# A Winograd-style 3x3 convolution: whole-image stores, whole-pair loads and one shared pool of 16 KB slots

## The chip, the cores and the metric

The kernel runs on one core of a Trainium2 chip. The metric is the device time of one execution in microseconds (us); lower is better. The kernel before takes 131.04 us, the median of 10 runs (130.84 to 131.21).

A core has five engines with a queue of instructions each: TensorE (PE in the profile, with its weight loads as PEld) multiplies matrices into eight PSUM banks; VectorE (DVE), ScalarE (ACT) and GpSimd (POOL) work element by element; SyncE (SP) issues transfers. Sixteen transfer engines move data between the chip's main memory (DRAM in the names) and SBUF, the memory on the core with 128 partitions. Transfers are issued here from SP, from ACT and from POOL; each of these has a queue of its own.

## The reference

The reference is a 3x3 convolution with zero padding, in fp32, on 16 images of 64 channels and 64 x 64 pixels, with 128 output channels:

```python
x_pad = np.pad(x, ((0, 0), (0, 0), (1, 1), (1, 1)), mode='constant')
for b in range(batch):
    for co in range(c_out):
        for ci in range(c_in):
            for kh in range(3):
                for kw in range(3):
                    output[b, co] += weight[co, ci, kh, kw] * x_pad[b, ci, kh:kh+h, kw:kw+w]
```

The input is 16.8 MB, the output 33.6 MB.

## The kernel before

**Tiling.** Two images make a pair: 2 x 64 input channels fill the 128 partitions. There are eight pairs (`NP`). A pair is computed in four blocks of eight double rows (16 output rows). Each image of the pair uses its own half of the partitions as contraction, so products for the two images alternate on PE.

**The arithmetic of a block.** Even and odd output rows share a part. With G0, G1 and G2 the weights of the three kernel rows, the kernel makes `U`, the product of G1 with the sum of the two rows of a double row (`ss`); `A`, the products of G2 - G1 (`G21`) and G0; and `Bt`, those of G0 - G1 (`G01`) and G2. The even output row is U + A and the odd one U + Bt. `group` issues the products: 6 for `U`, 12 for each of the other two, 30 a block. ACT copies `U` to SBUF as `ut` (L158), four buffers; DVE adds `A` and `ut` for both images (L163), then `Bt` and `ut` (L166), into the output tile `ot`. Then SP stores each image's 16 rows, 512 KB (L167), 4 KB in one piece per partition. `opool` has 16 such `ot` tiles of 8 KB per partition, which is four images' worth.

**Inputs.** All products use fp16. Pair 0 is loaded as fp32 (`x0`) in four cuts of rows, the first on ACT's queue and the rest on SP's, and ACT casts it to `xs[0]`. Pairs 1 to 7 are loaded by GpSimd's queue in halves (L56), with the cast done in the transfer. All eight fp16 pairs have a buffer of their own, so that no load waits for one. `load(p + 4)` is issued from GpSimd's program at the top of pair p.

**Row sums.** `ss` is made by DVE for pair 0 from `x0` and by GpSimd for the others from `xs` (L74), one pair ahead, in three buffers.

**Start.** The weights are loaded (SP), cast (L87), transposed by PE (L94) and combined into `Wt` by ACT and DVE (L96 to L104).

**Order.** A tile scheduler orders the program by engine and gives out the slots of the pools; `keep_in_program_order` (here `keep`) fixes the order of the calls it wraps. Every engine takes its instructions in order, and SP issues its transfers in order too. Each transfer on SP or ACT also uses one of eight completion semaphores in turn, and is issued when the earlier transfer on the same one has landed.

Of the kernel before, what the change touches and what calls it, by code (L numbers as in the profile page):

```python
# [8 lines left out]
F32 = mybir.dt.float32  # L9
F16 = mybir.dt.float16  # L10


@with_exitstack
def kernel(
    ctx: ExitStack,
    tc: tile.TileContext,
    x: bass.AP,
    weight: bass.AP,
    out: bass.AP,
):  # L20
    nc = tc.nc
    B, CI, H, W = x.shape
    CO = weight.shape[0]
    assert H == 64 and W == 64 and CI == 64 and CO == 128 and B % 2 == 0
    NP = B // 2
    RB = 8

    keep = tc.keep_in_program_order
    x_rows = x.rearrange("b c h w -> (b c) h w")
    out_rows = out.rearrange("b co h w -> b co h w")  # L30
    w_flat = weight.rearrange("co ci kh kw -> co (ci kh kw)")

    const = ctx.enter_context(tc.tile_pool(name="const", bufs=1))
    psum = ctx.enter_context(tc.tile_pool(name="psum", bufs=8, space=bass.MemoryType.PSUM))
    xpool = ctx.enter_context(tc.tile_pool(name="xpool", bufs=1))
    opool = ctx.enter_context(tc.tile_pool(name="opool", bufs=16))
    spool = ctx.enter_context(tc.tile_pool(name="spool", bufs=3))
    upool = ctx.enter_context(tc.tile_pool(name="upool", bufs=4))


    w_raw = const.tile([CO, CI * 9], F32)
    nc.sync.dma_start(w_raw, w_flat)  # L42
    x0 = const.tile([128, H, W], F32)
    xs = [
        xpool.tile([128, H, W], F16, tag=f"xs{p}", name="xs") for p in range(NP)
    ]
    cuts = [(0, 18), (18, 34), (34, 50), (50, 64)]
    for n, (lo, hi) in enumerate(cuts):
        eng = nc.scalar if n == 0 else nc.sync
        eng.dma_start(x0[:, lo:hi, :], x_rows[0:128, lo:hi, :])  # L50
    ident = const.tile([128, 128], F16)

    def load(p):
        for lo in (0, 32):
            keep(
                nc.gpsimd.dma_start(  # L56
                    xs[p][:, lo : lo + 32, :],
                    x_rows[128 * p : 128 * p + 128, lo : lo + 32, :],
                )
            )  # L60

    make_identity(nc, ident)
    for p in range(1, 4):
        load(p)


    ss = {}

    def sums(eng, p, src, lo, n):
        if p not in ss:  # L70
            ss[p] = spool.tile([128, H // 2, W], F16, tag="ss", name="ss")
        v = src.rearrange("p (j i) c -> p j i c", i=2)
        keep(
            eng.tensor_add(  # L74
                ss[p][:, lo : lo + n, :], v[:, lo : lo + n, 0, :], v[:, lo : lo + n, 1, :]
            )
        )


    Wt = const.tile([128, 5, 3, CO], F16)  # L80
    G0, G21, G1, G01, G2 = range(5)

    def wrow(i):
        return Wt[:, i, :, :].rearrange("p t c -> p (t c)")

    w16 = const.tile([CO, CI * 9], F16)
    nc.vector.tensor_copy(w16, w_raw)  # L87
    wps = {}
    for kh in (1, 2, 0):
        wp = psum.tile([128, 512], F32, tag="acc", name="wp")  # L90
        for k in range(3):
            t = 3 * kh + k
            for q in (0, 64):
                nc.tensor.matmul(wp[q : q + 64, k * CO : k * CO + CO], w16[:, t::9], ident)  # L94
        wps[kh] = wp[:, 0 : 3 * CO]
    keep(nc.scalar.copy(wrow(G1), wps[1]))  # L96
    sums(nc.vector, 0, x0, 0, RB)
    keep(nc.vector.tensor_sub(wrow(G21), wps[2], wrow(G1)))  # L98
    keep(nc.vector.tensor_sub(wrow(G01), wps[0], wrow(G1)))  # L99
    for n, (lo, hi) in enumerate(cuts):  # L100
        keep(nc.scalar.copy(xs[0][:, lo:hi, :], x0[:, lo:hi, :]))  # L101
        if n == 0:
            keep(nc.scalar.copy(wrow(G0), wps[0]))  # L103
            keep(nc.scalar.copy(wrow(G2), wps[2]))  # L104
        if n < 3:
            sums(nc.vector, 0, x0, RB * (n + 1), RB)

    for p in range(NP):
        if p + 1 < NP:
            for lo in (0, 16):  # L110
                sums(nc.gpsimd, p + 1, xs[p + 1], lo, 16)
        if p + 4 < NP:
            load(p + 4)
        for blk in range(4):
            j0 = blk * RB

            def group(wi_rows):

                tiles = [
                    psum.tile([128, RB, W], F32, tag="acc", name="acc") for _ in range(2)  # L120
                ]
                n = 3 * len(wi_rows)
                i = 0
                for wi, off in wi_rows:
                    for kw in (1, 0, 2):
                        c_lo, c_hi = max(0, 1 - kw), min(W, W + 1 - kw)
                        for b2 in range(2):
                            p0 = 64 * b2
                            lo, hi = j0, j0 + RB
                            if off is None:  # L130
                                rhs = ss[p][p0 : p0 + 64, lo:hi, c_lo + kw - 1 : c_hi + kw - 1]
                            else:
                                while 2 * lo + off < 0:
                                    lo += 1
                                while 2 * (hi - 1) + off > H - 1:
                                    hi -= 1
                                first = 2 * lo + off
                                last = 2 * (hi - 1) + off
                                rhs = xs[p][
                                    p0 : p0 + 64,  # L140
                                    first : last + 1 : 2,
                                    c_lo + kw - 1 : c_hi + kw - 1,
                                ]
                            nc.tensor.matmul(  # L144
                                tiles[b2][:, lo - j0 : hi - j0, c_lo:c_hi],
                                Wt[p0 : p0 + 64, wi, kw, :],
                                rhs,
                                start=i == 0,
                                stop=i == n - 1,
                            )  # L150
                        i += 1
                return tiles

            U = group([(G1, None)])
            us = []
            for b2 in range(2):
                ut = upool.tile([128, RB, W], F32, tag="ut", name="ut")
                nc.scalar.copy(ut, U[b2])  # L158
                us.append(ut)
            ots = [opool.tile([128, RB, 2, W], F32, tag="ot", name="ot") for _ in range(2)]  # L160
            A = group([(G21, 1), (G0, -1)])
            for b2 in range(2):
                nc.vector.tensor_add(ots[b2][:, :, 0, :], A[b2], us[b2])  # L163
            Bt = group([(G01, 0), (G2, 2)])
            for b2 in range(2):
                nc.vector.tensor_add(ots[b2][:, :, 1, :], Bt[b2], us[b2])  # L166
                nc.sync.dma_start(  # L167
                    out_rows[2 * p + b2, :, blk * 16 : blk * 16 + 16, :],
                    ots[b2].rearrange("p j i c -> p (j i) c"),
                )  # L170


# [28 lines left out]
```

## Time and profile before

| what | before |
|---|---|
| median of 10 runs | 131.04 us (130.84 to 131.21) |
| the profiled execution's own time | 130.91 us |
| its span | 129.1 us |
| PE busy (products) | 107.0 us, 83% |
| DVE busy | 86.8 us, 67% |
| ACT busy | 40.8 us, 32% |
| POOL busy | 37.7 us, 29% |
| moved by the transfer engines | 43.44 MB, mean 336 GB/s |
| read from and written to main memory | 17.07 and 33.55 MB, 392 GB/s over the span |
| stores, 64 of 512 KB, median from issue to landing | 10.5 us |
| loads with cast, 14 of 512 KB (as written), median to landing | 15.2 us |

The span is the time from the first to the last record of the profiled execution on the core; 1.8 us of the execution lie outside of it. The profile divides the span into 40 slices of 3.2 us and shows the busy share of each engine per slice in tenths, then the granted clock of PE, the share of the transfer engines, and the GB/s moved. For a load with cast the GB/s count the bytes written, half of those read. The chain of work that ended last is followed back from the last instruction; by line, half of the span on it is PE's products (L144) and 20% a store of `ot`.

### The profile page before, as it was taken

To read this page: it belongs to the slowest core of one execution; us is meant where nothing else is said; L and a number is where in the kernel's file an instruction comes from. 1 tells how busy PE (TensorE), PEld (TensorE's weight loads), DVE (VectorE), ACT (ScalarE), POOL (GpSimd) and SP (SyncE) were. 2 spreads that over 40 slices of the span, in tenths; PEclk is the share of its full clock that TensorE was granted. 3 is DMA by queue.
4 is the path that set the end of the run, shared out by engine and by line. 5 is a ranking of instruction groups with operands and counts; after the bars stand their busy time and mean duration, and the time that the engine had idled before them with its cause. 6 is when DMAs were issued, how large, how long until landed. Compare 5 with 4: busy or idle time off the path is not lost.

```text
span 129.1 us, 2506 instructions
## 1 busy us (share of the span) xinstructions
PE 107.0 (83%) x978; PEld 55.8 (43%) x978; DVE 86.8 (67%) x135; ACT 40.8 (32%) x72; POOL 37.7 (29%) x34
## 2 busy tenths in 40 slices
PE   0099269999999999898999999999999999995000
PEld 0053035555555555354555555555555555552000
DVE  0262599787778777169988777877777777778000
ACT  3084273333333333331333333333333333330000
POOL 7404699691049105700092009200000000000000
PEclk9999999999999999999999999999999999999755
DMA  3999999999999999999999999999999999999950
GB/s 73 361 287 269 242 204 222 274 277 279 277 273 279 286 273 278 287 414 420 415 414 424 412 420 416 412 420 420 414 415 420 418 419 412 419 418 418 420 245 14
DMA packets 11963, 43.44 MB, mean 336 GB/s; under 512 B 1328, under 2 KB 1328, under 8 KB 11952
## 3 DMA queue, kind: packets, MB, share of 16 engines
q1 hardware_dynamic: 9792, 35.36, 68.7%
q0 software_dynamic: 2016, 7.34, 28.1%
q10 hardware_dynamic: 144, 0.59, 1.4%
q8 instruction: 7, 0.11, 0.3%
q14 instruction: 4, 0.03, 0.1%
HBM read 17.07 MB, written 33.55 MB: 392 GB/s over the span
## 4 chain that ended last, share of the span: by engine, by line
PE 50%; DMA 31%; DVE 4%; issue 3%; ACT 2%; SPq 1%; ACTq 1%; DVEq 1%
PE acc L144 50%; DMA out_dram<-ot 20%; DMA x<-in_x_dram 10%; DVE ot L163 2%; ACT ut L158 1%; DVE ot L166 1%; ACT xs L101 1%; ACTq L196 1%; SPq L50 1%; DVEq L196 0%; SPq L42 0%; DVEq L163 0%; ACTq L158 0%
## 5 line engine op out<-in xcount | busy, mean ns | idle before, releaser
L144 PE MATMUL acc<-xs,Wt 64*128 64x504 f16 (+3 forms) x768 | 95.1, 378 | 4.8 <-ACT ut L158 3.4
L144 PEld LDWEIGHTS <-Wt 64*128 64x128 f16 x960 | 54.7, 95 | 55.5 <-issue 8.4
L163 DVE TENSOR_TENSOR ot<-acc,ut 128x512 f32<-128x512 f32 x64 | 41.5, 685 | 21.6 <-ACT ut L158 14.0
L158 ACT COPY ut<-acc 128x512 f32<-128x512 f32 x64 | 34.3, 589 | 65.7 <-issue 53.2
L74 POOL TENSOR_TENSOR ss<-xs 128x1024 f16<-128x1024 f16 x14 | 29.5, 2124 | 43.1 <-issue 26.4
L166 DVE TENSOR_TENSOR ot<-acc,ut 128x512 f32<-128x512 f32 x64 | 41.0, 683 | 0.0
L144 PE MATMUL acc<-ss,Wt 64*128 64x504 f16 (+1 forms) x192 | 32.4, 384 | 0.0
L74 DVE TENSOR_TENSOR ss<-x 128x512 f16<-128x512 f32 x4 | 5.4, 1350 | 4.5 <-DMA x<-in_x_dram 4.4
L56 POOL DMA_DIRECT2D xs<-in_x_dram x14 | 7.7, 561 | 0.1
L94 PE MATMUL wp<-ident,w 128*64 128x128 f16 x18 | 1.3, 328 | 6.3 <-DVE w L87 6.3
L101 ACT CAST xs<-x 128x1024 f16<-128x1024 f32 (+2 forms) x4 | 4.2, 1049 | 4.3 <-DMA x<-in_x_dram 4.3
L87 DVE CAST w<-w_raw 128x576 f16<-128x576 f32 x1 | 0.5, 460 | 5.8 <-DMA w_raw<-in_weight_dram 5.8
L94 PEld LDWEIGHTS <-w 128*64 128x64 f16 x18 | 1.1, 210 | 6.3 <-DVE w L87 6.3
L96 ACT CAST Wt<-wp 128x384 f16<-128x384 f32 x1 | 0.5, 479 | 4.5 <-PE wp L94 4.5
L96 ACT ACT_TABLE_LOAD x1 | 1.3, 1283 | 1.2 <-PEq L185 1.2
L98 DVE TENSOR_TENSOR Wt<-wp,Wt 128x384 f16<-128x384 f32 x1 | 0.6, 558 | 0.5 <-ACT Wt L96 0.5
L99 DVE TENSOR_TENSOR Wt<-wp,Wt 128x384 f16<-128x384 f32 x1 | 0.5, 547 | 0.0
L103 ACT CAST Wt<-wp 128x384 f16<-128x384 f32 x1 | 0.5, 479 | 0.0
L104 ACT CAST Wt<-wp 128x384 f16<-128x384 f32 x1 | 0.5, 484 | 0.0
masks.py:199 POOL TENSOR_SCALAR_AFFINE_SELECT ident<-ident 128x128 f16<-128x128 f16 x1 | 0.3, 294 | 0.1
masks.py:197 POOL MEMSET ident<- 128x128 f16 x1 | 0.2, 206 | 0.3 <-POOLq L185 0.3
L185 POOL MEMSET const-float32-0.0<- 128x1 f32 x1 | 0.1, 99 | 0.2 <-issue 0.2
(3 smaller groups left out, 0.3 us busy)
## 6 DMA issues: line engine op xcount, KB each, us to landing
out_dram<-ot SPq DMA_DIRECT2D x64, 512.0 KB, 10.5
xs<-in_x_dram POOLq DMA_DIRECT2D x14, 512.0 KB, 15.2
x<-in_x_dram SPq DMA_DIRECT2D x2, 512.0 KB, 8.7
x<-in_x_dram ACTq DMA_DIRECT2D x1, 576.0 KB, 5.5
x<-in_x_dram SPq DMA_DIRECT2D x1, 448.0 KB, 13.5
w_raw<-in_weight_dram SPq DMA_DIRECT2D x1, 288.0 KB, 5.0
```

The source lines that it names most:

```text
L50: eng.dma_start(x0[:, lo:hi, :], x_rows[0:128, lo:hi, :])
L56: nc.gpsimd.dma_start(xs[p][:, lo : lo + 32, :], x_rows[128 * p : 128 * p + 128, lo : lo + 32, :],)
L74: eng.tensor_add(ss[p][:, lo : lo + n, :], v[:, lo : lo + n, 0, :], v[:, lo : lo + n, 1, :])
L94: nc.tensor.matmul(wp[q : q + 64, k * CO : k * CO + CO], w16[:, t::9], ident)
L96: keep(nc.scalar.copy(wrow(G1), wps[1]))
L98: keep(nc.vector.tensor_sub(wrow(G21), wps[2], wrow(G1)))
L101: keep(nc.scalar.copy(xs[0][:, lo:hi, :], x0[:, lo:hi, :]))
L144: nc.tensor.matmul(tiles[b2][:, lo - j0 : hi - j0, c_lo:c_hi], Wt[p0 : p0 + 64, wi, kw, :], rhs, start=i == 0, stop=i == n - 1,)
L158: nc.scalar.copy(ut, U[b2])
L163: nc.vector.tensor_add(ots[b2][:, :, 0, :], A[b2], us[b2])
L166: nc.vector.tensor_add(ots[b2][:, :, 1, :], Bt[b2], us[b2])
L196: with _tile.TileContext(nc) as tc:
```

## The change

- **Loads.** All pairs are loaded as fp32 on SP's queue. Pair 0 comes in its four cuts, the others in one transfer each, 2 MB with 16 KB per partition. No load casts any more; `cast` does it on ACT in four pieces per pair, spread over the blocks of one to three pairs ahead of use (the lists `casts`). The weights' load goes to ACT's queue.
- **Row sums** on GpSimd are made from the fp32 pair.
- **Buffers.** A pool `big` has nine slots of 16 KB per partition. Incoming fp32 pairs (`xf`) and whole output images (`ot`) take them in turn. The fp16 pairs `xs` have three slots instead of eight.
- **Stores.** Both images of a pair are stored after its last block, each in one transfer of 2 MB with 16 KB per partition; the last pair in two halves per image.
- **Order on SP.** The source issues loads 0 to 5 at the start, load 6 at the end of pair 0 and load 7 at the end of pair 2, each ahead of the pair's stores. The scheduler takes the slots from those that are free.

The core of the diff, with the line numbers left out:

```diff
-    xpool = ctx.enter_context(tc.tile_pool(name="xpool", bufs=1))
-    opool = ctx.enter_context(tc.tile_pool(name="opool", bufs=16))
+    xpool = ctx.enter_context(tc.tile_pool(name="xpool", bufs=3))
+    big = ctx.enter_context(tc.tile_pool(name="big", bufs=9))
...
-    nc.sync.dma_start(w_raw, w_flat)
+    nc.scalar.dma_start(w_raw, w_flat)
...
     def load(p):
-        for lo in (0, 32):
+        xf[p] = big.tile([128, H, W], F32, tag="big", name="xf")
+        for lo, hi in cuts if p == 0 else [(0, H)]:
             keep(
-                nc.gpsimd.dma_start(
-                    xs[p][:, lo : lo + 32, :],
-                    x_rows[128 * p : 128 * p + 128, lo : lo + 32, :],
+                nc.sync.dma_start(
+                    xf[p][:, lo:hi, :], x_rows[128 * p : 128 * p + 128, lo:hi, :]
                 )
             )
+    def cast(p, n):
+        if p not in xs:
+            xs[p] = xpool.tile([128, H, W], F16, tag="xs", name="xs")
+        lo, hi = cuts[n]
+        keep(nc.scalar.copy(xs[p][:, lo:hi, :], xf[p][:, lo:hi, :]))
+    def outs(p):
+        ots[p] = [big.tile([128, H // 2, 2, W], F32, tag="big", name="ot") for _ in range(2)]
+    for p in range(5):
+        load(p)
+    outs(0)
+    load(5)
...
+    pieces = lambda q: [(q, n) for n in range(4)]
+    casts = {p: [] for p in range(NP)}
+    casts[0] = pieces(1)
+    casts[1] = pieces(2) + pieces(3)[:2]
+    casts[2] = pieces(3)[2:] + pieces(4)
+    casts[3], casts[4], casts[5] = pieces(5), pieces(6), pieces(7)
...
-            for lo in (0, 16):
-                sums(nc.gpsimd, p + 1, xs[p + 1], lo, 16)
-        if p + 4 < NP:
-            load(p + 4)
+        if p not in ots:
+            outs(p)
+        for q, _ in dict.fromkeys((q, 0) for q, _ in casts[p]):
+            if q not in ss:
+                for lo in (0, 16):
+                    sums(nc.gpsimd, q, xf[q], lo, 16)
...
-                nc.scalar.copy(ut, U[b2])
+                keep(nc.scalar.copy(ut, U[b2]))
...
+            if p == 0 and blk < 3:
+                cast(0, blk + 1)
+            c = casts[p]
+            for q, n in c[len(c) * blk // 4 : len(c) * (blk + 1) // 4]:
+                cast(q, n)
...
-                nc.sync.dma_start(
-                    out_rows[2 * p + b2, :, blk * 16 : blk * 16 + 16, :],
-                    ots[b2].rearrange("p j i c -> p (j i) c"),
-                )
+            if blk == 3 and p == 0:
+                outs(1)
+                load(6)
+                outs(2)
+            if blk == 3 and p == 2:
+                load(7)
+            parts = {3: (0, 64)} if p < NP - 1 else {1: (0, 32), 3: (32, 64)}
+            if blk in parts:
+                lo, hi = parts[blk]
+                for b2 in range(2):
+                    keep(nc.sync.dma_start(
+                        out_rows[2 * p + b2, :, lo:hi, :],
+                        ots[p][b2].rearrange("p j i c -> p (j i) c")[:, lo:hi, :],
+                    ))
```

## The prediction

> **What bounds the kernel now.** I read the page's slices first, then stretches, the chain in order of time, the waits, and the timeline where a wait is long.
>
> ```profile
> DMA  3999999999999999999999999999999999999950
> ...
> q1 hardware_dynamic: 9792, 35.36, 68.7%
> q0 software_dynamic: 2016, 7.34, 28.1%
> ```
>
> The transfer engines are busy from slice 1 to slice 37. q1 is SP's queue (stores, most of pair 0), q0 GpSimd's casting loads of pairs 1 to 7: 28.1% of 129.1 us is 36.3 us for 14.68 MB read.
>
> ```profile
> 37.00:54.00 17.00, 17.00 (x164) 9.00 (x160) 11.27 (x18) 6.37 (x12) 9.25 (x6) 1.00 1.06 276
> ...
> 90.00:100.00 10.00, 10.00 (x98) 5.28 (x96) 7.90 (x13) 3.66 (x8) 0.00 (x0) 1.00 1.03 417
> ```
>
> Stretches: busy us of PE, PEld, DVE, ACT, POOL, then clock, DMA share, GB/s. Both resources are full: PE has no hole, DMA share is at 1. In stores alone 417 GB/s over 16 engines is 157 ns per 4 KB row.
>
> ```profile
> 27.96 26.30 DMA out_dram<-ot
> ...
> 54.38 0.69 DVE L163 TENSOR_TENSOR ot<-acc,ut 128x512 f32<-128x512 f32 x1 [2.64 <-DMA out_dram<-ot]
> ...
> 55.13 1.45 PE L144 MATMUL acc<-xs,Wt 64*128 64x512 f16 x11 [0.87 <-DVE ot L163]
> ```
>
> First line from the chain, the others from the timeline. A store issued at 27.96 lands at 54.26, since loads share the engines; only then has DVE a free output buffer. PE stands with full PSUM and goes on 0.87 us after the landing. This costs little today, but the change makes it large.
>
> ```profile
> 40.09 1.07 ACT L158 COPY ut<-acc 128x512 f32<-128x512 f32 x2 [2.09 <-issue]
> 52.90 1.07 ACT L158 COPY ut<-acc 128x512 f32<-128x512 f32 x2 [2.09 <-issue]
> ```
>
> ```profile
> 8.78 4.30 PE L144 MATMUL acc<-xs,Wt 64*128 64x512 f16 x24
> 60.68 2.95 PE L144 MATMUL acc<-xs,Wt 64*128 64x512 f16 x24
> ```
>
> Timeline again. Four blocks lie between the two copies: PE needs 12.81 us per pair, 3.2 per block. The same 24 products take 4.30 us early and 2.95 later: PE starts slow.
>
> **What the Trainium skill says.** "DMA: Bandwidth & Descriptors", Queues, rings and completion order: each transfer engine takes descriptors in ring order. The trace agrees: stores land in order of issue, up to 26.4 us after it. The same page, Why small descriptors are slow, has a fixed few cycles per packet; Where 436 GB/s comes from, a ceiling of 435 GB/s. The packet records give 93 ns for rows of 2,304 B, 159 for 4,096 and 178 for 4,608: a line with a small constant. "TensorE: Matmul & The Clock Gate", Part 1: PE runs at half clock until a window of some 3.4 us was busy, and falls back after an idle one. The trace agrees: after PE's last product, near 118.0, the clock record falls to 0.5 at 121.3.
>
> **The change, part by part.**
>
> *Loads without cast, 16 KB rows.* On the line above a 16 KB row takes 604 to 612 ns; starts of 4 KB rows follow each other 4 ns closer than they last, so 605, my estimate. Ends: 602 by the skill's ceiling, 628 if a row is moved as four of today's. A pair is 8 rows per engine: 4.84 us. Seven loaded pairs cost 33.9 us instead of 36.3, sixteen images of stores 77.4 instead of 16 × 32 × 157 ns = 80.4.
>
> *Order on SP.* This decides. The build's order on SP is: pair 0 in four cuts, pairs 1 to 6 whole, stores of pairs 0 and 1, load 7, the other stores. Load 6 stands late in the source, but the scheduler gives it the ninth, unused slot. Loads 4, 5 and 6 wait for nothing but the landing of the weights and of the first two cuts (their completion semaphores are reused), all before about 9 us. So six whole pairs lie in the ring ahead of the first store.
>
> Working, us from the span's start. Full flow from about 2.6 (0.16 MB had moved by 3.0). Weights and pair 0: 8 × (93+178+159+159+153) ns, less 4 ns each: 5.8, to 8.4. Six pairs: 29.0, to 37.4. Pair 0's two stores: 9.7, to 47.1. The slowest engine lands some 1.1 later than the middle one (landing records at 54 to 90 us): S = 48.2.
>
> *The buffers.* In the built program pair 2's two outputs take the slots of pair 0's outputs, and DVE waits for those stores. Pair 2 gets there long before: weights land as today near 5.7, first products at 7.5; block 0 is as slow as today. ACT's in-order queue then holds the cast of pair 1's first quarter ahead of block 1's copies, and waits for that load: 8.4 + 4.84 + 1.1 = 14.3. Its 1.15 us and the casts behind it put PE's end of pair 0 near 23.5, pair 1 near 36.3, and DVE's first add of pair 2 near 38. Image 0's slot is free at 43, image 1's at S. DVE stands, with everything behind it. PE fills the eight banks with U, A, B of two blocks (6.5 us) and stops near 43. The PE gain of the start (today's stall from 13.7 to 17.1 goes) is lost here.
>
> *After S.* PE goes on at S + 0.9 = 49.1 (the 0.87 above). Two blocks of pair 2 remain, paced by DVE's backlog of adds of 0.68 us: 6.9, to 56.0. PE stood 6 us, almost surely a whole window, so it restarts at half clock for 3.4 to 6.8 us (at the start, from 6.3 to the clock record's first entry at 12.06): it loses half of that, less 0.5 that the pacing hides. Ends 0 and 2.9; I take 2.0: 58.0. Pairs 3 to 6, 4 × 12.81 = 51.2: 109.2.
>
> *Tail.* Transfers have caught up by then: pair 5's stores end near 108. Pair 6's first image is ready 0.6 after PE (DVE's last adds at today's end), 109.8; data flow 1.4 after issue (as from 0.74 at the start), 111.2. From here 8.39 MB: pair 6 whole, pair 7 in halves, 4 × 4.84 = 19.4, to 130.6. Pair 7 is computed by 122.9 and queues. Slowest engine 1.1, then 1.0 from last landing to end (today 128.1 to 129.1): 132.7.
>
> *Costs hidden.* ACT gains 28 casts of 1.05: 4 × 1.07 + 4.2 = 8.5 of 12.81 per pair; only in pairs 0 to 2 is it near full, under the slack before S. If that cover went, a U copy would wait at most one cast, 1.15. POOL reads fp32: "GPSIMD Engine Reference", 3.1 gives 4.5 us for 2,048 fp32, by estimate 2.25 for ours, beside 2.12 in the trace; two per pair. POOL's load issues (14 × 0.56) go. Weights move to ACT's queue, cut 0 to SP's: between nothing and 0.5 us, hidden ahead of S. Fewer resident fp16 pairs (three): a slot comes free when PE has left the pair three before. The later output slots: pair 3 needs store 1a, landed near 53; pair 5 needs pair 2's, near 73, asked at 84. No further wait.
>
> Against the profiled execution: span 129.1, 1.8 around it, 130.91; the median of the runs is 131.04, 0.1 above. 132.7 + 1.8 = **134.5 us**.
>
> **Rivals.**
>
> *Stores aren't held (faster, and the change's aim).* If the stores of pair 0 landed before about 41, PSUM would absorb the wait and transfers alone would set the end: 2.6 + 5.8 + 33.9 + 77.4 = 119.7, + 1.1 + 1.0 + 1.8 = 123.6. It decides if at least two of the six loads came behind the stores in the ring, or the two directions didn't wait for each other. For: a big transfer saves 3%, and PE starts 3 us earlier. Against: SP's order in the build, and the 26.3 us store above.
>
> *The stall without the half clock.* PE's idle stretch has one product in it when image 0's slot comes free, and could count as active: 132.5, and 131.0 to 131.5 with 602 ns and a start and slowest engine 0.5 better each. For: today's 3.4 us hole at 13.7 didn't lower the clock. Against: that hole is half as long.
>
> *No gain from longer rows.* 628 ns instead of 605: S is 64 × 0.023 = 1.5 later, the tail 0.7: 136.7; with an engine as late as today's at the end (2.8 behind the middle one) 138.4.
>
> **How the numbers follow.** Likeliest case 0.66, 134.5, own range 132 to 137; stall without half clock 0.15, 131 to 132.5; rows no faster or a late engine 0.09, 136.5 to 138.5; stores not held 0.10, near 123.6. About 0.2% (0.26 us) is what a measurement of this kernel tells from no change. Slower takes the first three cases but 0.04 of the second: 0.86; same 0.03; faster 0.11 with the rival. The range 130.9 to 137.4 leaves out that rival and the upper end.
>
> **What would show it.** Pair 0's stores issued near 25, landing only at 43 and 48; DVE's longest wait, some 5 and 4 us, for a store at the first adds of pair 2; PE empty from about 43 to 49, then 24 products in some 5 us with clock 0.5; DMA slices full to about 70, then holes before each pair's stores; GB/s near 430 where stores run alone. Wrong if pair 0's stores land before 41, if SP holds loads back, if PE's hole is under 3 us, or if the end comes more than 26 us after PE leaves pair 6 (23.5 in the sum).

## The result and the profile after

The changed kernel takes 137.66 us, the median of 9 runs (136.78 to 138.03), against 131.03 before on the same chips: a ratio of 1.0501 (95% interval 1.0487 to 1.0514). It is slower, by the mechanism forecast, and 3.2 us above the forecast of 134.5; the upper end of the range, 137.4, lies 0.26 below it. The profiled execution took 137.05, of which the span is 135.3.

Two slips of the description above: an `ot` tile of the kernel before holds 4 KB per partition, not 8 ("four images' worth" for 16 of them is right), and the casts of pairs 1 to 7 run one or two pairs ahead of use, never three.

Each transfer leaves sixteen landing records, one per transfer engine. Below, a transfer has landed with the last of them; "on the middle engine" means their median. The records do not say which engine is which.

First the slices of the page after, and its two main queues (share of the 16 transfer engines' span on the right):

```profile
PEclk9999968999999965899999999999999999999755
DMA  4999999999999999999994999299739955999992
...
q1 hardware_dynamic: 4176, 50.33, 88.2%
q10 hardware_dynamic: 144, 0.29, 0.9%
```

Before, the transfer engines were busy in every slice from 1 to 37. Now they are busy up to slice 20 (near 70 us) and then have holes. The casting queue is gone, and q1 (SP's) carries loads and stores alike. The clock row has a dip at slices 14 to 16 (and a smaller one at 5 and 6: the clock record has 0.5 from 17.77 to 21.19, after a hole of 1.62 us in PE at 14.86; PE later waits for the stores anyway, so this one is hidden).

The stretches (busy us of PE, PEld, DVE, ACT, POOL, with counts; then granted clock, DMA share, GB/s):

```profile
45.00:50.00 5.00, 0.37 (x1) 0.09 (x1) 0.86 (x2) 0.97 (x1) 0.00 (x0) 0.85 0.99 426
50.00:55.00 5.00, 4.58 (x22) 1.82 (x23) 4.04 (x7) 0.76 (x2) 0.00 (x0) 0.50 0.99 421
...
90.00:95.00 5.00, 5.00 (x50) 2.49 (x48) 3.54 (x6) 3.77 (x6) 0.00 (x0) 1.00 0.98 419
95.00:100.00 5.00, 5.00 (x50) 2.49 (x48) 4.27 (x8) 2.53 (x5) 0.00 (x0) 1.00 0.51 213
```

From 45 to 50 no computing engine works for even 1 of the 5 us, while the transfers are full; the next 5 us have 22 products at a clock of 0.50, where a full stretch has 50. Later the roles are swapped: PE is full, and the share of the transfers drops, to 0.51 in the last of these stretches.

The chain in order of time (start, length, what) names the cause, and the timelines of DVE and PE show it:

```profile
27.71 21.84 DMA out_dram<-ot
...
50.42 72.89 PE acc L161 x638
```

```profile
44.85 0.69 DVE L184 TENSOR_TENSOR ot<-acc,ut 128x512 f32<-128x512 f32 x1 [4.36 <-DMA out_dram<-ot]
49.68 0.69 DVE L184 TENSOR_TENSOR ot<-acc,ut 128x512 f32<-128x512 f32 x1 [4.14 <-DMA out_dram<-ot]
```

```profile
42.77 1.65 PE L161 MATMUL acc<-xs,Wt 64*128 64x512 f16 x12
45.59 0.37 PE L161 MATMUL acc<-xs,Wt 64*128 64x512 f16 x1 [1.17 <-DVE ot L184]
50.42 2.72 PE L161 MATMUL acc<-xs,Wt 64*128 64x512 f16 x11 [4.46 <-DVE ot L184]
...
53.81 3.71 PE L161 MATMUL acc<-xs,Wt 64*128 64x512 f16 x24
```

Pair 0's second store is issued at 27.71 and lands at 49.55. DVE's first add of pair 2 for image 0 waits 4.36 us for the first store (landed 44.73), the one for image 1 another 4.14 for the second. PE runs out of PSUM at 44.4, does one product, and goes on at 50.42: 0.87 after the landing, as in the kernel before, where the hole was 0.87 long and is now 6 us.

The gain that the change aims at did come. By the packet records, the rows of one transfer engine add up, on average over the sixteen, to 125.8 us before and 120.2 after (16 KB rows take 611 ns, median; 8 KB rows of casting loads took 322, 4 KB rows 159). It does not show in the time, because from near 70 us on the transfers have holes, in which they wait for PE.

### The profile page after: what moved, and what is told of

It is laid out like the page before. It is cut to its first block, busy times and chain, and to the rows that moved or that the text cites. A ratio compares the mean times of both kernels' runs of the same rounds, so it can differ in the third digit from the quotient of the medians.

```text
span 135.3 us, 2438 instructions
## 1 busy us (share of the span) xinstructions
PE 110.3 (82%) x978; PEld 54.7 (40%) x978; DVE 84.1 (62%) x135; ACT 67.2 (50%) x100; POOL 33.5 (25%) x20
## 3 DMA queue, kind: packets, MB, share of 16 engines
HBM read 17.07 MB, written 33.55 MB: 374 GB/s over the span
## 4 chain that ended last, share of the span: by engine, by line
PE 60%; DMA 16%; DVE 3%; ACT 1%; issue 1%; DVEq 0%
PE acc L161 60%; DMA out_dram<-ot 16%; DVE ot L184 2%; DVE ot L187 1%; ACT xs L61 1%; DVEq L227 0%; ACT ut L175 0%; DVEq L184 0%
## 5 line engine op out<-in xcount | busy, mean ns | idle before, releaser
L161 PE MATMUL acc<-xs,Wt 64*128 64x504 f16 (+3 forms) x768 | 98.0, 384 | 7.4 <-DVE ot L184 5.6
L161 PEld LDWEIGHTS <-Wt 64*128 64x128 f16 x960 | 53.6, 97 | 62.5 <-issue 14.5
L85 POOL TENSOR_TENSOR ss<-xf 128x1024 f16<-128x1024 f32 x14 | 32.8, 2366 | 54.5 <-issue 32.9
L61 ACT CAST xs<-xf 128x1024 f16<-128x1024 f32 (+2 forms) x32 | 33.2, 1058 | 2.8 <-DMA xf<-in_x_dram 2.8
L161 PE MATMUL acc<-ss,Wt 64*128 64x504 f16 (+1 forms) x192 | 34.3, 400 | 0.0
L85 DVE TENSOR_TENSOR ss<-xf 128x512 f16<-128x512 f32 x4 | 2.6, 683 | 0.0
```

The source lines that it names most:

```text
L61: keep(nc.scalar.copy(xs[p][:, lo:hi, :], xf[p][:, lo:hi, :]))
L85: eng.tensor_add(ss[p][:, lo : lo + n, :], v[:, lo : lo + n, 0, :], v[:, lo : lo + n, 1, :])
L161: nc.tensor.matmul(tiles[b2][:, lo - j0 : hi - j0, c_lo:c_hi], Wt[p0 : p0 + 64, wi, kw, :], rhs, start=i == 0, stop=i == n - 1,)
```

## The experiments

The theory: six loads stand ahead of pair 0's stores in SP's ring, a slot is released only when a whole image has landed, and so DVE stalls; the stall is long enough to cost PE its clock; the coarse stores then lengthen the tail. The main rival: the loss comes from somewhere else that the change brought (casts on ACT, the end of the kernel, the size of the stores), and the order of the ring has little to do with it.

### How many loads stand ahead of the stores

Load 6 moved behind pair 0's stores:

```diff
                 outs(1)
-                load(6)
-                outs(2)
...
+            if blk == 3 and p == 0:
+                load(6)
+                outs(2)
```

> Load 6 is issued behind pair 0's two stores instead of ahead of them; nothing else is changed. Theory (ring order): five whole pairs lie ahead of the first store instead of six, so image 1's store lands one load (4.88 us) earlier, near 44.7 instead of 49.55. DVE's second wait in pair 2 shrinks from 4.1 us to about 3, PE's hole from 6 us to about 1.5, too short for the half clock, and pair 2 loses some 1.5 us instead of 9: 129 to 131 us. Rival 1 (the 28 casts on ACT slow the blocks down): no change, 137 us. Rival 2 (whole-image stores lengthen the tail): no change beyond 0.5 us, 137 us.

Measured: 131.9 us (131.48 to 132.39), ratio 1.0071 (1.004 to 1.0102), 0.9 above the expected stretch, and 5.8 below the changed kernel. In the other kernel load 5 also comes behind pair 0's stores, and load 6 behind pair 1's:

```diff
     outs(0)
-    load(5)
...
-                load(6)
-                outs(2)
...
+            if blk == 3 and p == 0:
+                load(5)
+                outs(2)
+            if blk == 3 and p == 1:
+                load(6)
```

> Load 5 behind pair 0's stores and load 6 behind pair 1's; four whole pairs ahead of the first store. Theory: image 1's store lands near 39.5, before DVE asks for its slot at 41; no store is waited for, PE has no hole, PE leaves pair 7 near 116.5 and the transfers end near 125: 128 to 129.5 us, less than the kernel before. From five pairs to four little is left to gain (1 us), from six to five much (7 us): the effect is a threshold and not a slope. Rivals 1 and 2: 137 us.

Measured: 128.75 us (128.43 to 130.06), ratio 0.9849 (0.9795 to 0.9904): as expected, and faster than the kernel before. So with six, five and four whole pairs ahead of the first store the time is 137.66, 131.9 and 128.75. The same bytes move through the same nine slots in all three; the casts on ACT, the whole-image stores and the end of the kernel are unchanged. In all three programs pair 2's outputs take the slots of pair 0's outputs, so it is the same wait each time. In the third the stores have landed at 35.24 and 40.06, DVE waits for no store, and its first adds of pair 2 stand here:

```profile
42.15 1.29 DVE L183 TENSOR_TENSOR ot<-acc,ut 128x512 f32<-128x512 f32 x2 [0.61 <-ACT ut L174]
```

One reservation: the scheduler also orders the two images' U products differently, in one block of the second build and in three of the third, and in the traces products of U then stand between those of `Bt`. But in the later pairs the stores are issued 12.81 us apart per pair in all three, so this order gives PE no other pace.

With load 6 moved, the chain has the store and then PE:

```profile
25.87 18.87 DMA out_dram<-ot
...
45.62 72.17 PE acc L161 x638
```

Image 1's store lands at 44.75 instead of 49.55: one load of 4.8 us less in front of it. DVE's wait in that timeline reads:

```profile
44.87 0.69 DVE L184 TENSOR_TENSOR ot<-acc,ut 128x512 f32<-128x512 f32 x1 [4.14 <-ACT xs L61]
```

The line names a cast of ACT, but the add starts 0.12 after the landing, and 0.12 is also what lies between landing and add in the kernel after (44.73 and 44.85). The chain names the store, and in this program the slot of image 1 is the one that this store frees. PE's hole is 2.36 us here, and yet the clock fell to 0.5 from 45.70 to 49.12. I had counted on it to hold; the half clock costs 1.7 us here (below), more than the 0.9 by which I was off.

### The stores without the ring, the loads without the stores

The store half of the change alone: the kernel before, with its casting loads on GpSimd's queue, and four output slots of a whole image.

```diff
-    opool = ctx.enter_context(tc.tile_pool(name="opool", bufs=16))
+    opool = ctx.enter_context(tc.tile_pool(name="opool", bufs=4))
...
+        ots = [opool.tile([128, H // 2, 2, W], F32, tag="ot", name="ot") for _ in range(2)]
         for blk in range(4):
...
-            ots = [opool.tile([128, RB, 2, W], F32, tag="ot", name="ot") for _ in range(2)]
```

The stores are then issued after block 3, as in the changed kernel.

> The kernel before with its casting loads on GpSimd's queue, and of the change only the stores: whole images of 2 MB (last pair in halves), four image slots in the same 64 KB. Loads and stores lie in two rings, so no store stands behind all loads, but a slot comes free only when a whole image has landed. Theory of ring order alone: no stall, 130 to 132 us. Theory that a whole image per slot is enough: pair 0's stores start near 28, share the engines with the loads until some 54, land near 47; DVE wants the slots near 41, and stands 6 us: 133 to 136 us. I expect the second.

Measured: 135.15 us (134.95 to 135.39), ratio 1.0317 (1.0301 to 1.0332), as the second theory has it. Rows of the timelines of DVE, then of PE:

```profile
48.37 0.69 DVE L163 TENSOR_TENSOR ot<-acc,ut 128x512 f32<-128x512 f32 x1 [5.07 <-DMA out_dram<-ot]
63.24 0.69 DVE L163 TENSOR_TENSOR ot<-acc,ut 128x512 f32<-128x512 f32 x1 [3.80 <-DMA out_dram<-ot]
```

```profile
49.11 1.45 PE L145 MATMUL acc<-xs,Wt 64*128 64x512 f16 x11 [3.16 <-DVE ot L163]
63.98 1.45 PE L145 MATMUL acc<-xs,Wt 64*128 64x512 f16 x11 [1.89 <-DVE ot L163]
```

PE's two holes are 5.05 us together; the kernel before has 0.87 there. The difference, 4.2, is about the loss of 4.1. It is not the whole account of the profiled execution: PE ends 5.05 us later there than in the kernel before (at 123.07 instead of 118.02), since its start is slower too (0.5 in the clock record from 17.07 to 20.48, after a hole that is 0.4 longer), and the end after PE is 0.5 shorter. So a whole image per slot is enough for a stall even where loads and stores use different queues: a block's store can leave as soon as that block is done and frees its tile for a later block, while an image's store has to wait for block 3 and frees nothing before its last byte. That the ring's order adds to the stall is what the runs with five and four loads show; this run shows that it is not the only cause. The prediction had put all of it on the ring.

The other half: loads and casts as after, but five load slots and the 16 `ot` tiles and block stores of before.

```diff
-    big = ctx.enter_context(tc.tile_pool(name="big", bufs=9))
+    big = ctx.enter_context(tc.tile_pool(name="big", bufs=5))
+    opool = ctx.enter_context(tc.tile_pool(name="opool", bufs=16))
...
+            ots[p] = [opool.tile([128, RB, 2, W], F32, tag="ot", name="ot") for _ in range(2)]
...
+                keep(nc.sync.dma_start(
+                    out_rows[2 * p + b2, :, blk * 16 : blk * 16 + 16, :],
...
+            if blk == 3 and p + 5 < NP:
+                load(p + 5)
```

> Of the change only the loads: fp32 pairs of 2 MB on SP's queue and the casts on ACT, five fp32 slots; stores by block and image of 512 KB from sixteen slots of 4 KB per partition, as before. Four whole pairs lie ahead of the first store, the others come after the stores of the pair five before. Theory: a slot comes free with each block, no stall; transfers run from 2.6 to some 124 without a hole and the last store is small: 126 to 128.5 us. If the casts on ACT or the fp32 loads cost time by themselves: over 131 us.

A miss: 132.2 us (132.08 to 132.6), ratio 1.0096 (1.0078 to 1.0114). By its size it would fit the rival, that casts or fp32 loads cost time by themselves; the trace has the computing engines done 15 us before the end. There is no stall of note in the waits (engine, line, releaser: total, times, longest):

```profile
DVE ot L182 <- DMA out_dram<-ot: 3.0, 3, 2.4
...
PE acc L158 <- DVE ot L182: 0.4, 1, 0.4
```

DVE's last add ends near 115 in a span of 130.5. The casts are thus not what sets the time. The transfers go on: the last store has landed on the middle engine at 125.9, on the fifteenth at 127.1 and on the last at 129.45. The loads' rows save less than I had counted (35.0 us per engine against 36.2 for the casting loads, by the packet records), the 4 KB store rows save nothing, and one engine comes 3.5 us after the middle one. This kernel is bound by transfers and by that engine, and its fp32 loads alone bring nothing.

### What the half clock costs

Extra products, whose results are thrown away, between `A` and `Bt` of block 1 of pair 2, where PE runs dry; first 20 of them, then 36.

```diff
+            if p == 2 and blk == 1:
+                for _ in range(20):
+                    nc.tensor.matmul(
+                        U[0],
+                        Wt[0:64, G1, 1, :],
+                        ss[p][0:64, j0 : j0 + RB, :],
...
             Bt = group([(G01, 0), (G2, 2)])
```

> Twenty extra products (results thrown away, into a bank that has been copied and is not read again) stand on PE between the groups A and Bt of block 1 of pair 2, where PE is idle for 6 us; some 4.3 us of work in the hole. Everything else is as in the changed kernel. Theory: the clock isn't lowered (record 1.0 from 48 to 55), pair 2 ends 2 to 2.5 us earlier, the whole by as much: 135 to 135.7 us. If the half clock costs nothing beside DVE's backlog: 137.5 us. If the extra products delay PE: over 138.

> As the run with 20 extra products, but 36, so that the whole hole of 6 to 8.4 us on PE is filled (36 x 0.216 = 7.8 us). With 20, PE stood empty for another 3.7 us before image 1's slot came free, one whole clock window, and the clock fell as before. Theory: with no empty window the clock stays at 1.0; PE goes on within 0.5 us of the store's landing, and the time is 2 to 3 us below the run with 20, 1 to 2.5 us below the changed kernel: 135 to 136.5 us. If the half clock costs nothing: 138 to 139 us, as with 20.

With 20: 138.95 us (138.57 to 139.16), ratio 1.0607 (1.0572 to 1.0641), a miss. With 36: 135.91 (135.86 to 136.22), ratio 1.0379 (1.0362 to 1.0397), as expected. PE's timeline with 20 and then with 36:

```profile
42.59 4.48 PE L187 MATMUL acc<-ss,Wt 64*128 64x512 f16 x20
...
50.97 2.72 PE L161 MATMUL acc<-xs,Wt 64*128 64x512 f16 x11 [3.69 <-DVE ot L184]
```

```profile
42.27 7.93 PE L187 MATMUL acc<-ss,Wt 64*128 64x512 f16 x36
...
50.76 1.45 PE L161 MATMUL acc<-xs,Wt 64*128 64x512 f16 x11 [0.34 <-DVE ot L184]
...
58.25 0.38 PE L161 MATMUL acc<-ss,Wt 64*128 64x512 f16 x1
```

Twenty products only move the hole: it is then 3.69 us long and the clock falls at 49.72 all the same. Thirty-six fill it; the clock stays at 1.0, and eleven products take 1.45 instead of 2.72. The cost of the half clock can then be read off the chain, whose last long piece is the same 638 products in each build: 72.89 us after, 73.22 with 20 extra, 70.49 with 36, and 72.17 with load 6 moved. So the half clock costs 2.4 us in the changed kernel and 1.7 with load 6 moved. Of the 2.4 the medians show 1.75 and the profiled spans 1.1, since PE goes on 0.34 later with 36 extra products and the last store's slowest engine lies 1.9 behind the middle one in both builds with extra products, but 0.9 after. With 20, that (1.0), a restart 0.55 later and 0.33 of longer products make up the 1.8 by which the span with 20 extra products exceeds that of after.

### The tail, and a second ring

All images stored in two halves of 1 MB; loads 6 and 7 move in the source so that their places in the ring stay, and a slot still holds a whole image:

```diff
     load(5)
+    load(6)
...
                 outs(1)
-                load(6)
                 outs(2)
-            if blk == 3 and p == 2:
+            if blk == 0 and p == 2:
                 load(7)
-            parts = {3: (0, 64)} if p < NP - 1 else {1: (0, 32), 3: (32, 64)}
+            parts = {1: (0, 32), 3: (32, 64)}
```

> All images are stored in two halves of 1 MB (8 KB per partition), not the last pair's alone; load 6 is issued at the start and load 7 ahead of pair 2's stores as in the changed kernel, so the order of loads and stores in the ring stays. Theory: the two waits of pair 2 stay (image 0's slot now free near 47, image 1's at 49.6), PE's hole stays, but when PE leaves pair 6 half of it has been stored: the last 3 transfers' worth in place of 4 no longer wait in line, and the end is set by pair 7's second half, 1.0 + 1.1 + 4.9 + 2 us after PE's last product: 134 to 135.5 us. Rival 2 (the tail is the main loss): below 132. Rival 1: 137.

Measured: 135.3 us (134.72 to 135.52), ratio 1.0324 (1.0291 to 1.0356), as expected. DVE still waits 8.74 and 1.74, and PE goes on at 50.84, no sooner than after (50.42). What gets shorter is the end: from the end of PE's last product to the end of the span 8.4 us instead of 10.6, as pair 6's first halves leave while it is still computed. Some 2.1 us of the time after are thus the coarse end. Smaller stores alone do not shorten the stall; smaller slots were not tried here.

Pair 0's two stores issued from ACT's queue, and nothing else moved:

```diff
+            if p == 1 and blk == 0:
+                for b2 in range(2):
+                    keep(nc.scalar.dma_start(
+                        out_rows[b2, :, :, :],
+                        ots[0][b2].rearrange("p j i c -> p (j i) c"),
+                    ))
...
-            if blk in parts:
+            if blk in parts and p > 0:
```

> As the changed kernel, but pair 0's two image stores are issued from ScalarE's own queue instead of SyncE's, so that they do not stand behind loads 4 to 6 in SyncE's ring; bytes, buffers and all other issues are unchanged. Theory (the order in one ring holds the stores): the transfer engines alternate between two rings from about 28 us on, image 0's store lands near 38 instead of 44.7 and image 1's near 44 to 48 instead of 49.5, TensorE's hole before pair 2's block 1 gets shorter, and the time is 134 to 136.5. Rival (it is not the ring but the transfer engines' common backlog, served first come first served): 44.7 and 49.5 stay, and so does the time, 137 to 138.

Measured: 138.12 us (137.87 to 139.6), ratio 1.0539 (1.0523 to 1.0554). Both theories miss. DVE's waits are:

```profile
41.93 0.69 DVE L190 TENSOR_TENSOR ot<-acc,ut 128x512 f32<-128x512 f32 x1 [1.51 <-DMA out_dram<-ot]
51.70 0.69 DVE L190 TENSOR_TENSOR ot<-acc,ut 128x512 f32<-128x512 f32 x1 [9.08 <-DMA out_dram<-ot]
```

Image 0's store lands at 41.81, 2.9 earlier, so SP's order did hold it; image 1's lands at 51.58, 2.0 later. From 30.8 on the two rings share each engine about evenly: loads 5 and 6 land 9.7 us apart instead of 4.9. On its middle engine load 6 is through at 46.6, and pair 1's first store follows it in SP's ring; image 1's store is through at 50.3. If pair 1's store takes half of the flow in those 3.7 us, that is 1.9, about the delay of image 1's store on the middle engine (48.5 to 50.3). The Trainium skill, "DMA: Bandwidth & Descriptors", Queues, rings and completion order, says that a transfer engine goes round robin between its rings; the trace agrees. A second ring is thus not a way past a backlog. The slot that decides is the second, and its store has to have fewer bytes ahead of it in either ring.

### What bounds the kernel without the stall

The version with four loads ahead, and the same with pairs 5 and 6 stored in halves and pair 7 by blocks:

```diff
+            parts = {3: (0, 64)}
+            if p >= 5:
+                parts = {1: (0, 32), 3: (32, 64)}
+            if p == NP - 1:
+                parts = {b: (16 * b, 16 * b + 16) for b in range(4)}
```

> The run with four pairs ahead of the first store, and in addition pairs 5 and 6 stored in halves and pair 7 by block. Theory: with no stall left, what remains is the hole of some 3 us in the transfers before pair 6's whole images, and the last transfers in line; both go: 125.5 to 127 us. If the transfers themselves are the limit all along (no hole that counts): 128.5 us, no change.

> The kernel of loads4 again, beside the next one on the same chip: load 5 behind pair 0's stores and load 6 behind pair 1's. Theory (the hole near the end of transfers costs only what the slowest transfer engine would cost anyway): 128.5 to 129. Rival (the hole costs its whole length): over 0.8 above the next kernel.

> The kernel of fine_end again: loads4 with pairs 5 and 6 stored in halves and pair 7 by blocks, so that no hole in transfers is left. Theory (bound by transfers and their slowest engine): 128.2 to 128.7, at most 0.4 below loads4. Rival: 127.5 or less, as span 126.6 of the first profile would give.

The finer end alone gave 128.47 us (128.36 to 129.35), ratio 0.9821 (0.9788 to 0.9854): above the expected stretch, and what the rival named there (128.5, no change). Side by side on one chip, the coarse end takes 128.52 (128.42 to 129.78), ratio 0.9827 (0.9799 to 0.9855), and the finer one 129.2 (128.64 to 129.65), ratio 0.986 (0.9836 to 0.9883). The first is as expected, the second 0.5 above its stretch. The finer one is not faster; the intervals overlap. Slices of the page with the coarse end, then with the finer one:

```profile
DMA  4999999999999999999999999999999939999992
```

```profile
DMA  3999999999999999999999999999999999999970
```

The hole at slice 32 is closed and nothing is won. The last store has landed on the middle engine at 126.1 with the coarse end and at 124.3 with the finer one, but on the slowest at 127.0 and 126.75: the engine that is late has 0.9 us of arrears after a hole and 2.4 without one. A hole would be time in which it catches up; that fits these numbers and was not tried by itself. So in these two executions the coarse end is bound by PE, for which the transfers wait before pair 6's stores, and then by the last stores, and the fine end by the transfers of the slowest engine.

Both are among the slower executions of their kernels (129.78 and 129.65). In both the clock record has 0.5 for one stretch near the start (17.91 to 21.32, and 17.59 to 21.00). In the first profile of the fine end (128.4) it has not, PE ends 1.17 us sooner than in the second, and the last store lands at 125.67 instead of 126.75, though neither has a hole in the transfers; why, is open. Why one engine is late I can't say from these runs; the kernel before had one 2.8 late.

Either of these versions beats both kernels, by 1.4 to 1.8% against the kernel before.

## Why the prediction was right and wrong

**Right in sign and mechanism.** SP's order, six pairs ahead of the stores, is what the runs with five and four show. The stores landed at 44.73 and 49.55 ("at 43 and 48"), DVE's waits were 4.36 and 4.14 ("some 5 and 4"), PE was empty but for one product from 44.4 to 50.4 ("about 43 to 49"), the clock was at 0.5 when it went on, and the transfers were full to about 70. Three rivals are ruled out by the profile: the stores were held; the stall came with the half clock, for one product in the hole did not save it; and the 16 KB rows were faster, 611 ns and not 628. The costs put at nothing held: after the stall the pace is 12.81 us per pair, from pair 3's first product at 60.31 to pair 7's at 111.54, with the casts on ACT.

Two things were not foreseen. Whole-image slots stall DVE by themselves, without loads ahead in the ring (135.15 us). And PE came to pair 2 at 38.97, not near 36.3, held up in part by the early half clock (where that stretch is missing, as with 36 extra products, it came at 37.17); that this error cost nothing is luck, since the store was not there yet.

**The steps that failed: terms of the sum.** The path was right, and four of its terms were too small; S, the landing of the store that ends the stall, was off most. Against the predicted span of 132.7 the measured one is 2.6 longer:

| step, as predicted | predicted | measured | more |
|---|---|---|---|
| S, landing of image 1's store | 48.2 | 49.55 | 1.35 |
| from S to pair 3 | 9.8 | 10.76 | 0.96 |
| pairs 3 to 6 | 51.2 | 51.23 | 0.0 |
| tail, from pair 7's first product to the end | 23.5 | 23.76 | 0.26 |

- *Full flow from about 2.6, then 5.8 for weights and pair 0.* That flow was through at 9.4 on the middle engine, not 8.4. The sum used the median rows, 93 and 178 ns for the weights and the first cut. On average they take 152 and 257 ns in this trace, and took 182 and 218 in the kernel before. With the averages of all five transfers the 5.8 becomes 6.9. The engines are not idle meanwhile: their share is 0.93 from 3 to 4 us and 1.00 or more from 4 on. The eight transfers after it took 4.88 instead of 4.84 each, 0.3 to 0.4 together.
- *PE fills the eight banks with U, A, B of two blocks.* It got one group less far. Eight banks hold four groups of two images. U of block 0 is copied out by ACT, but the banks of A of block 0, whose adds wait, are the ones that `Bt` of block 1 needs. So two and a half blocks were left, not two: 7.5 us at full clock, by the run with 36 extra products, where the sum had 6.9.
- *I take 2.0* for the half clock, between 0 and 2.9: it is 2.4.
- The run's median lies 0.6 above the profiled execution; the sum, from the kernel before, allowed 0.1. What these executions have more of is open.

The four misses have one sign, and together (2.6 and 0.6) are the 3.2 us. The range's end, 137.4, was too near: it was worked out from the bounds of the rows and from a late transfer engine, with the half clock left at its middle value and the start of the flow taken as exact.

**A rival's size.** "It decides if at least two of the six loads came behind the stores in the ring" is confirmed in sign, since with two behind there is no stall. But the size, 123.6, was not reached: such a kernel takes 128.5 to 128.75. The sum had 1.1 for the slowest engine, taken from a stretch before, and let the transfers alone set the end. In the profiled executions the last landing is at 125.67 to 127.3: by PE's chain with the coarse end, and with arrears of 2.4 where there is no hole.

## What to carry to other kernels

When a buffer is freed by a store, count the bytes that stand ahead of that store, in its own ring and in any other that is busy: that count, divided by the rate, is how long the store is put off. What of it lies behind the moment at which the slot is asked for is the stall, and prefetching as far as slots allow makes it longer. One load moved in the source (load 6 behind the stores) was worth 5.8 us, and two moved loads turned a loss of 5% into a gain of 1.5 to 1.7%. A larger transfer also delays the release of its buffer to its last byte, so give it slots for what is computed in the meantime, or leave it small.

## What the runs showed of the hardware

- The clock can fall after a hole that is shorter than a window. The clock record changes in steps of 3.41 us: its half-clock stretches in the middle of these kernels last 3.41, 6.83 or 10.24. With load 6 moved, the window from 42.29 to 45.70, counted in these steps, holds about 1.0 us of products at its beginning, and the clock is 0.5 in the next. The Trainium skill, "TensorE: Matmul & The Clock Gate", Part 1, speaks of an idle window of some 3.4 us; here a mostly idle one was enough. Counted so in all the traces here, while the clock is at 1.0, every window with at most 1.2 us of products is followed by 0.5 and every one with at least 1.8 by 1.0; between 1.5 and 1.7 both occur, so the share alone does not decide there. Where a hole lies counts as much as its length: the 3.38 us hole of the kernel before (at 13.73) falls into two windows with 1.7 us of products each, and the clock stays; the 1.62 us hole after (at 14.86) lies in one window with 1.7, and the clock falls. Twenty products at the beginning of an 8 us hole helped nothing: the window from 46.30 to 49.72 then holds 1.0.
- At the last store the slowest of the sixteen transfer engines is 2.4 to 3.5 us behind the middle one in kernels whose transfers never pause (2.4 with the fine end, 2.8 before, 3.5 with fp32 loads and block stores), and 0.1 to 1.9 behind where there are pauses (0.1 with all stores in halves, 0.9 after, 1.9 with extra products).
- Rows of 4, 8 and 16 KB take 159, 309 and 611 ns, those of 4 and 16 KB in loads and stores alike: a quarter of the 16 KB row is 153 ns, 4% less than a 4 KB row.
